# A fixed TensorE order re-spaced: where norm, the raw inputs and the fill steps stand, and when x is requested

## The chip, the core and the metric

The kernel runs on one core of a Trainium2 chip. A core has a matrix engine (TensorE, PE in the profile), a vector engine (VectorE, DVE), a scalar engine (ScalarE, ACT), a general engine (GpSimd, POOL) and SyncE (SP), which here issues the DMAs. Each engine works through its own queue in order; they wait for each other at semaphores. The metric is device time in microseconds.

## What is computed

One decoder layer with two branches beside each other, on x of 1024 rows by 1024 columns. The cut-down reference:

```python
h = rms_norm(x, pre_norm_gain)
proj = h @ w_in                                   # q, k, v of 3 attention groups, gates, RWKV inputs
# branch A: dilated sliding-window attention on q, k, v -> o_attn
# branch B: RWKV-7
pr = pr + (pr_prev - pr) * rwkv_shift_mix         # token shift, gives r, k, v, w_low, a_low
decay = exp(-exp(-softplus(-(w0 + tanh(w_low) @ w_up)) - 0.5))
a = sigmoid(a0 + a_low @ a_up)
kk = k * k_k;  kk = kk / max(norm(kk per head), 1e-12)
k = k * (1 + (a - 1) * k_a)
y = rwkv7_scan(r, decay, k, v, -kk, kk * a)       # delta-rule state update, token by token
o_rwkv = group_norm(y) * ln_w + ln_b + (sum(r * k * r_k)) * v
# merge
y_attn = (o_attn * silu(z_attn)) @ w_up_attn;  y_rwkv = (o_rwkv * silu(z_rwkv)) @ w_up_rwkv
merged = sigmoid(g_attn) * y_attn + sigmoid(g_rwkv) * y_rwkv
x = x + rms_norm(merged @ w_out, post_norm_gain)
```

## The kernel before

The work runs in stages: an opening (`start`), a small bias table, the RWKV branch (`rwkv`), attention, and the merge (`finish`).

The opening loads x in eight tiles of 128 rows, each by two DMAs that SP requests (L250, L251); the nine vectors of the layer (gains, mixes and so on) come by nine small DMAs into one tile `rows` (`vec_rows`, L298), which PE transposes once (L261). Each x tile is squared and summed (on ScalarE for the first four tiles, L276), scaled on DVE to `xn`, transposed by PE (L285), and split into a high part `hh` and a low part `hl` (L286, L287). All projections are then three fp32r matmuls per block of 128 rows of w_in: hi by hh, hi by hl, lo by hh. A weight block is requested by SP into `wstage`, its high part made on ScalarE or DVE (L135, L137) and the low part `wlo` on POOL (L138).

In the RWKV stage the sequence is cut into eight segments of 128 tokens. A segment has a preparation (`rwkv_prep`), transposed rows (`rwkv_rows`), the recurrence (`rwkv_chain`) and a group norm (`rwkv_post`), each written as a generator that does a step and yields. The steps of a preparation are:

- 1: requests of the raw k and r inputs of the segment, and their token shift on ScalarE and DVE (L506, L508);
- 2: the low-rank products (`wa` by `waup`), ScalarE's `sig` and `aa`, DVE's scan `c` (L528), POOL's `cm` (L529), ScalarE's `kk` and q = kk squared (L535);
- 3, called norm here: PE multiplies q by a head selector `hs`, DVE takes the maximum with 1e-24 into `rn` (L542), POOL raises it to the power -1/2 (L543);
- 4: PE transposes `rn`, DVE copies it to `rt` (L553), POOL makes `k`, half of `bk` and half of `ar`;
- 5: PE spreads `rt` over the heads, DVE and POOL finish `kk`, `ar` (L567) and `bk` (L569), `r` and the two `bw` tiles;
- 6 and 7: PE multiplies `ar` by `bk` into `gt` for half of the heads each, DVE evacuates with a mask (L590). Behind step 7 come the shift of v and `rwkv_blocks`: gt goes to DRAM (`tin_d`) and comes back as 16 by 16 blocks (`xinv`), 28 dependent DVE instructions (L617, L619) invert them, and they go to DRAM and back again (`x_d`, `xd`), where DVE transposes them to `xt` (L639);
- 8 to 11: PE completes the inverse (`pi`) from xt and gt.

`rwkv_rows` transposes `bw` for the two chunks of a segment (evacuated by ScalarE to `bkt`, L680 to L682), then v and r. `rwkv_chain` has for each of the two chunks three steps: rhs, upd (evacuated to `uv`, L724 on DVE and L725 on ScalarE), and snew.

PE has a fixed order through the whole RWKV stage (`keep_in_program_order`), written by hand: small steps with fill steps between them. A fill step is one matmul step of a projection that is due anyway (a pair of 256-column matmuls for the first 384 steps, then one of 512 columns), so that PE has work while the other engines answer. The order comes from three tables:

- `PROLOGUE`: pairs (what, number of fill steps behind it), before the loop over segments. "0", "1", "2" are the next step of that segment's preparation, "f" the next step of the first segment's rows. The first "0" is step 1 of segment 0, the second step 2, and so on.
- `LOOP`: pairs (what, weight), gone through once for each segment i. "C" is the next step of the chain, "f" of the next segment's rows, "t", "e", "a", "b" the next step of the preparation of segments i, i+1, i+2, i+3, "h" of the last segment's group norm. Behind each entry stand weight times `FILLS[i]` fill steps.
- `FILLS`: the number of fill steps per unit of weight, for each of the eight segments.

What is left of the fill steps after the loop follows in a row. On all other engines and queues the order is made by a scheduler that sees the whole program.

Of the kernel before, what the change touches and what calls it, by code (L numbers as in the profile page):

```python
# [34 lines left out]
C = 64  # L35
# [7 lines left out]

PROLOGUE = (("0", 24), ("0", 10), ("0", 10), ("0", 8), ("0", 44), ("0", 4), ("0", 4), ("1", 12), ("1", 16), ("1", 12),
            ("f", 4), ("f", 4), ("1", 8), ("1", 24), ("0", 8), ("0", 8), ("0", 8), ("1", 4), ("1", 6), ("0", 6), ("2", 0),
            ("f", 8))
LOOP = (("C", 0), ("t", 0), ("f", 1), ("a", 1), ("h", 1), ("C", 0), ("f", 1), ("a", 2), ("C", 0), ("a", 1), ("h", 2),
        ("C", 0), ("a", 1), ("f", 0), ("e", 2), ("C", 2), ("a", 1), ("e", 0), ("C", 1), ("a", 1), ("e", 1), ("b", 0))  # L50
FILLS = 6 * [6] + [5, 3]
CPS = SEG // C
KAPPA = math.exp(-0.5)
NEG = -1.0e30
# [58 lines left out]
class Kernel:  # L113
# [103 lines left out]
    def start(self):  # L217
        nc, tc, ctx, a = self.nc, self.tc, self.ctx, self.a
        pool = lambda **k: ctx.enter_context(tc.tile_pool(**k))
        self.cst = cst = pool(name="cst", bufs=1)  # L220
        self.wst = pool(name="wst", bufs=3)
        self.whl = pool(name="whl", bufs=3)
        self.ev = pool(name="ev", bufs=2)
        self.acc = pool(name="accp", bufs=2, space=PSUM)
        self.dram = pool(name="dram", bufs=1, space=DRAM)
        self.hstack = ExitStack()
        self.hpool = self.hstack.enter_context(tc.tile_pool(name="hT", bufs=1, side="right"))
        self.w_in = a["w_in"][0]
        self.sstack = ExitStack()
        self.small = self.sstack.enter_context(tc.tile_pool(name="small", bufs=1))  # L230

        self.ident = cst.tile([P, P], F32, name="ident")
        make_identity(nc, self.ident)
        self.eps = cst.tile([P, 3], F32, name="eps")
        nc.vector.memset(self.eps[:, 0:1], RMS_EPS)
        nc.vector.memset(self.eps[:, 1:2], GN_EPS)
        nc.vector.memset(self.eps[:, 2:3], 0.0)

        self.vecs = cst.tile([P, 49], F32, name="vecs")
        warm = cst.tile([P, 1], F32, name="warm")  # L240
        nc.scalar.activation(warm, self.eps[:, 2:3], AF.Sqrt)

        self.hT = []
        xr = a["x"][0].rearrange("(i r) d -> r i d", r=16)
        with tc.tile_pool(name="xin", bufs=1) as xin, tc.tile_pool(name="xps", bufs=5, space=PSUM) as xps:
            tiles = []

            def load(t):
                x = xin.tile([P, D], F32, name="x", tag="x", bufs=8)
                nc.sync.dma_start(x[0:64], xr[2 * t])  # L250
                nc.sync.dma_start(x[64:128], xr[2 * t + 1])  # L251
                tiles.append(x)

            rows = xin.tile([49, P], F32, name="rows")
            self.vec_rows(rows)
            for t in range(8):
                load(t)
                if t == 3:
                    self.w_wa = self.load_split(self.w_in, KT, OFF_WA)
            ps = xps.tile([P, 512], F32, name="xT", tag="xT")  # L260
            nc.tensor.transpose(ps[:, 0:49], rows, self.ident[0:49, 0:49])  # L261
            nc.vector.tensor_copy(self.vecs, ps[:, 0:49])
            self.small_loads()
            for half in range(2):
                hh = self.hpool.tile([P, KT, 512], F32R, name=f"hh{half}")
                hl = self.hpool.tile([P, KT, 512], F32R, name=f"hl{half}")
                self.hT.append((hh, hl))
                xs = []
                for j in range(4):
                    x = tiles[half * 4 + j]  # L270
                    sq = xin.tile([P, D], F32, name="sq", tag="sq", bufs=2)
                    st = xin.tile([P, 2], F32, name="st", tag="st", bufs=4)
                    if half:
                        nc.vector.tensor_tensor_reduce(sq, x, x, 1.0, 0.0, ALU.mult, ALU.add, st[:, 0:1])
                    else:
                        nc.scalar.activation(sq, x, AF.Square, accum_out=st[:, 0:1])  # L276
                    nc.scalar.activation(st[:, 1:2], st[:, 0:1], AF.Sqrt, bias=self.eps[:, 0:1], scale=1.0 / D)
                    nc.vector.reciprocal(st[:, 0:1], st[:, 1:2])
                    xn = xin.tile([P, D], F32, name="xn", tag="xn", bufs=5)
                    nc.vector.tensor_scalar(xn, x, st[:, 0:1], None, ALU.mult)  # L280
                    xs.append(xn)
                for k in range(KT):
                    ps = xps.tile([P, 512], F32, name="xT", tag="xT")
                    for j in range(4):
                        nc.tensor.transpose(ps[:, j * P:(j + 1) * P], xs[j][:, k * P:(k + 1) * P], self.ident)  # L285
                    nc.scalar.activation(hh[:, k], ps, AF.Copy, scale=self.gain[:, k:k + 1])  # L286
                    nc.vector.scalar_tensor_tensor(hl[:, k], ps, self.gain[:, k:k + 1], hh[:, k].bitcast(F32),  # L287
                                                   ALU.mult, ALU.subtract)
# [51 lines left out]
    def rwkv(self):  # L340
# [5 lines left out]
        with ExitStack() as ctx:  # L346
# [72 lines left out]
            def run(n):  # L419
                for _ in range(n):  # L420
                    next(fill, None)
# [4 lines left out]
            rows = self.rwkv_rows(0)  # L426
            for g, n in PROLOGUE:
                next(rows if g == "f" else prep[int(g)])
                run(n)
            for i in range(NSEG):  # L430
# [3 lines left out]
                work = dict(t=prep[i], e=prep[i + 1], a=prep[i + 2], b=prep[i + 3], f=rows, h=post)  # L434
                for g, n in LOOP:
                    if g == "C":
                        with tc.high_priority():
                            next(chain)
                    else:
                        next(work[g], None)  # L440
                    run(n * FILLS[i])
                for n in range(3 * i, 3 * i + 3):
# [712 lines left out]
```

## Time and profile before

| what | value |
|---|---|
| median of 3 runs | 1426.84 us (1419.84 to 1430.86) |
| the profiled execution's own time | 1421.31 us |
| its span | 1419.5 us |
| PE busy | 1333.9 us, 94% |
| DVE, ACT, POOL busy | 55%, 41%, 33% |
| mean granted TensorE clock | 0.986 |
| opening | 0 to about 36 us |
| prologue of the RWKV stage | about 92 to 185 us |
| loop over the eight segments | about 185 to 560 us, some 49 us a segment |

The profile is one execution, recorded by hardware. A row of a timeline has the start, the duration, the engine and line, the operation, and in brackets how long the engine had stood idle before it and what ended that. A row of the waits has an engine with its instruction, what it waited for, the sum, the number and the longest. The granted clock is 1.00 at 2.4 GHz and 0.50 at 1.2 GHz.

### The profile page before, as it was taken

The numbers are of one execution on the slowest core, as the hardware profiler recorded it, in microseconds if no ns is written. First come the engines' busy times: TensorE is split into PE (matmuls) and PEld (weight loads), VectorE is DVE, ScalarE is ACT, GpSimd is POOL, SyncE is SP. The second block draws the span as 40 slices with busy tenths as digits, with TensorE's granted clock in tenths as the row PEclk, the third lists the DMA queues.
The fourth block names the chain that finished last, engine by engine and source line by source line (L and its number), as shares of the span: only waits on it lengthen the run. The fifth ranks groups of instructions, "written<-read, shape, count | busy, mean of one in ns | idle before, by whom it ended". The sixth has DMA issues, their size and how long they took to land. (4 is left out here: it accounts for less than half of the span.)

```text
span 1419.5 us, 25770 instructions
## 1 busy us (share of the span) xinstructions
PE 1333.9 (94%) x10079; PEld 1115.3 (79%) x10079; DVE 779.9 (55%) x1676; ACT 576.4 (41%) x1378; POOL 475.4 (33%) x378
## 2 busy tenths in 40 slices
PE   5989899989999999999989998999899998999997
PEld 3989889767777777888878887888678876777886
DVE  5312657556464523565676557655766577338523
ACT  4444665564565332354425432643354320003211
POOL 1335644553355232322132213312222234433300
PEclk9999999999999999999999999999999999999999
DMA  7673544422322223111131112211221145654216
GB/s 175 184 217 107 135 107 101 114 68 74 100 77 74 62 75 94 45 41 34 43 101 35 48 40 75 62 44 41 62 67 31 45 152 176 200 169 150 62 38 171
DMA packets 192912, 131.17 MB, mean 92 GB/s; under 512 B 46421, under 2 KB 173022, under 8 KB 192790
## 3 DMA queue, kind: packets, MB, share of 16 engines
q1 hardware_dynamic: 192790, 129.52, 32.8%
q8 instruction: 79, 1.29, 0.4%
q14 instruction: 43, 0.35, 0.1%
HBM read 100.31 MB, written 33.89 MB: 95 GB/s over the span
## 5 line engine op out<-in xcount | busy, mean ns | idle before, releaser
L142 PE MATMUL acc<-hh,whi 128*128 128x512 f32 (+1 forms) x1360 | 480.3, 376 | 24.3 <-DVE kl L855 10.7
L142 PE MATMUL acc<-hh,wlo 128*128 128x512 f32 (+1 forms) x1360 | 470.2, 369 | 0.6 <-POOL wlo L138 0.6
L142 PE MATMUL acc<-hl,whi 128*128 128x512 f32 (+1 forms) x1360 | 470.0, 369 | 0.4 <-DVE hl L287 0.4
L138 POOL TENSOR_TENSOR wlo<-wstage,whi 128x512 fp32r<-128x512 f32 x186 | 247.6, 1332 | 527.2 <-DVE whi L135 244.1
L142 PEld LDWEIGHTS acc<-hh,whi 128*128 128x128 f32 x1360 | 246.8, 192 | 71.0 <-issue 15.8
L142 PEld LDWEIGHTS acc<-hh,wlo 128*128 128x128 f32 x1360 | 246.8, 191 | 38.7 <-POOL wlo L138 0.8
L142 PEld LDWEIGHTS acc<-hl,whi 128*128 128x128 f32 x1360 | 247.3, 192 | 36.2 <-issue 1.1
L875 ACT ACTIVATE L<-L,nm 128x128 f32<-128x128 f32 (+1 forms) x192 | 84.4, 441 | 86.1 <-DVE nm L872 85.8
L869 DVE CUSTOM_DVE_ANT_0 L<-pw,bias 128x128 f32<-128x128 f32 (+1 forms) x192 | 62.2, 350 | 50.3 <-PE pw L868 49.7
L854 POOL CAST k<-k 64x512 fp32r<-64x512 f32 x48 | 48.7, 1015 | 106.8 <-ACT k L853 98.2
L135 DVE CAST whi<-wstage 128x512 fp32r<-128x512 f32 x108 | 52.3, 486 | 51.3 <-PE acc L142 32.5
L853 ACT CAST k<-acc 64x512 fp32r<-64x512 f32 x48 | 43.0, 896 | 75.1 <-DVE kl L855 51.7
L137 ACT CAST whi<-wstage 128x512 fp32r<-128x512 f32 x78 | 48.6, 623 | 55.6 <-PE acc L142 24.7
L845 ACT ACTIVATE q<-acc 64x512 fp32r<-64x512 f32 x48 | 44.0, 916 | 56.1 <-DVE q L846 29.5
L855 DVE TENSOR_TENSOR kl<-acc,k 64x512 fp32r<-64x512 f32 x48 | 45.6, 950 | 33.5 <-ACT k L853 33.1
L617 DVE TENSOR_TENSOR xtmp<-xinv 64x14 f32<-64x14 f32 (+6 forms) x112 | 32.3, 288 | 46.7 <-DMA xinv<-tin_d 43.9
L846 DVE SCALAR_TENSOR_TENSOR q<-acc,q 64x512 fp32r<-64x512 f32 x48 | 45.0, 937 | 22.5 <-ACT q L845 21.6
L945 ACT CAST ph<-pw 128x512 fp32r<-128x512 f32 x72 | 40.9, 583 | 36.3 <-PE pv L954 22.0
L946 DVE TENSOR_TENSOR pl<-pw,ph 128x512 fp32r<-128x512 f32 x72 | 47.3, 670 | 11.9 <-ACT ph L945 10.6
L868 PE MATMUL pw<-kl,q 128*128 128x128 f32 (+1 forms) x192 | 50.6, 278 | 1.2 <-DVE kl L855 1.2
L1096 PE MATMUL acc<-wo,mh 128*128 128x512 f32 x128 | 50.4, 394 | 0.0
L1095 PE MATMUL acc<-wo,mh 128*128 128x512 f32 x128 | 50.2, 392 | 0.0
(232 smaller groups left out, 2173.7 us busy)
## 6 DMA issues: line engine op xcount, KB each, us to landing
wstage<-in_w_in_dram SPq DMA_DIRECT2D x170, 256.0 KB
x<-in_x_dram SPq DMA_DIRECT2D x32, 256.0 KB
raw<-raw_d SPq DMA_DIRECT2D x24, 258.0 KB
raw_d<-rv SPq DMA_DIRECT2D x24, 256.0 KB
wb<-wd SPq DMA_DIRECT2D x24, 256.0 KB
bias_d<-bias_r SPq DMA_DIRECT2D x24, 192.0 KB
tb_d<-tb SPq DMA_DIRECT2D x16, 256.0 KB
ga_d<-tb SPq DMA_DIRECT2D x16, 256.0 KB
```

What stands on the lines that cost most here:

```text
L135: self.nc.vector.tensor_copy(hi, x)
L137: self.nc.scalar.copy(hi, x)
L138: self.nc.gpsimd.tensor_tensor(lo, x, hi.bitcast(F32), ALU.subtract)
L142: ins = self.nc.tensor.matmul(*args, **kw)
L854: nc.gpsimd.tensor_copy(self.gview(ks2[h][b], g, half), hi.bitcast(F32))
L855: nc.vector.tensor_tensor(self.gview(kl[h][a], g, half), pv, hi.bitcast(F32), ALU.subtract)
L868: nc.tensor.matmul(ps[:, :w], qs2[h][:, qc], kl[h][:, kc], start=False, stop=True)
L869: nc.vector.tensor_tensor_reduce(l[:, l0:l0 + w], ps[:, :w], self.bias[h][:, bo:bo + w], 1.0, -3.0e38, ALU.add, ALU.max, st[:, gi, 0, h, n ...
L875: nc.scalar.activation(ls, ls, AF.Exp, bias=nm[:, n:n + 1], scale=1.0, accum_out=st[:, gi, 1, h, n:n + 1])
L946: nc.vector.tensor_tensor(pl[:, :cw], ps[:, :cw], ph[:, :cw].bitcast(F32), ALU.subtract)
L1095: nc.tensor.matmul(ps, mh[k][:, ts], wh[:, k], start=k == 0, stop=False)
L1096: nc.tensor.matmul(ps, mh[k][:, ts], wl[:, k], start=False, stop=False)
```

## The change

```diff
-PROLOGUE = (("0", 24), ("0", 10), ("0", 10), ("0", 8), ("0", 44), ("0", 4), ("0", 4), ("1", 12), ("1", 16), ("1", 12),
-            ("f", 4), ("f", 4), ("1", 8), ("1", 24), ("0", 8), ("0", 8), ("0", 8), ("1", 4), ("1", 6), ("0", 6), ("2", 0),
+PROLOGUE = (("0", 40), ("0", 16), ("0", 24), ("0", 8), ("0", 30), ("0", 8), ("0", 8), ("1", 20), ("1", 14), ("1", 12),
+            ("f", 12), ("1", 8), ("f", 4), ("1", 16), ("0", 8), ("0", 8), ("0", 8), ("1", 6), ("1", 6), ("0", 6), ("2", 0),
             ("f", 8))
-LOOP = (("C", 0), ("t", 0), ("f", 1), ("a", 1), ("h", 1), ("C", 0), ("f", 1), ("a", 2), ("C", 0), ("a", 1), ("h", 2),
-        ("C", 0), ("a", 1), ("f", 0), ("e", 2), ("C", 2), ("a", 1), ("e", 0), ("C", 1), ("a", 1), ("e", 1), ("b", 0))
-FILLS = 6 * [6] + [5, 3]
+LOOP = (("C", 0), ("t", 0), ("f", 1), ("a", 1), ("h", 1), ("C", 0), ("a", 1), ("f", 2), ("C", 0), ("a", 1), ("h", 2),
+        ("C", 0), ("a", 1), ("f", 0), ("e", 2), ("C", 0), ("b", 2), ("a", 1), ("e", 0), ("C", 1), ("a", 1), ("e", 1))
+FILLS = 4 * [6] + [6, 5, 4, 3]
...
             rows = xin.tile([49, P], F32, name="rows")
-            self.vec_rows(rows)
             for t in range(8):
                 load(t)
+                if t == 1:
+                    self.vec_rows(rows)
                 if t == 3:
                     self.w_wa = self.load_split(self.w_in, KT, OFF_WA)
```

Five things are in it. The nine vector requests stand behind x's second tile. The prologue's numbers of fill steps are other ones, 270 in all instead of 232, and one step of segment 1's preparation stands between the two first steps of rows. In the loop, norm (the second "a") stands directly behind the second chain step, before the second half of bw, with the two weights exchanged. The raw inputs of segment i+3 ("b") are requested behind the fifth chain step instead of at the end of the slot. `FILLS` has 5 and 4 for the sixth and seventh segment instead of 6 and 5. The number of fill steps is the same, 1056; 38 more stand in the prologue, 36 fewer in the two segments, two fewer behind the loop. From line 258 on, line numbers of the changed kernel are one higher.

On PE, in a segment of the loop, the steps behind the second chain step, upd (acc is a fill step, bw the transposes of the second chunk, hs,q is norm), stand so before:

```order
L142 MATMUL upd<-rhs_s,tt_440 64x64 x8
L148 MATMUL pg<-ident,bw 128x128 x4
L142 MATMUL acc<-hh_239,whi 128x512
L142 MATMUL acc<-hl_240,whi 128x512
L142 MATMUL acc<-hh_239,wlo 128x512
L142 MATMUL acc<-hh_153,whi 128x512
L142 MATMUL acc<-hl_154,whi 128x512
L142 MATMUL acc<-hh_153,wlo 128x512
L142 MATMUL pg<-hs,q 128x2 x4
```

and so in the changed kernel:

```order
L142 MATMUL upd<-rhs_s,tt_440 64x64 x8
L142 MATMUL pg<-hs,q 128x2 x4
L142 MATMUL acc<-hh_239,wlo 128x512
L142 MATMUL acc<-hh_239,whi 128x512
L142 MATMUL acc<-hl_240,whi 128x512
L142 MATMUL acc<-hh_239,wlo 128x512
L142 MATMUL acc<-hh_239,whi 128x512
L142 MATMUL acc<-hl_240,whi 128x512
L142 MATMUL pg<-ident,bw 128x128 x4
```

Norm's four small products have moved ahead of six fill steps and of bw's four transposes.

On DVE, at the same place of a segment, the maximum of rn (L542) and the copy uv of upd stand among the last instructions of an inverse (xtmp, xinv) so before:

```order
L724 COPY uv<-upd 64x4x64
L619 TENSOR_TENSOR xinv<-xinv,xtmp 64x10x5
L617 TENSOR_TENSOR xtmp<-xinv 64x44
L619 TENSOR_TENSOR xinv<-xinv,xtmp 64x11x4
L617 TENSOR_TENSOR xtmp<-xinv 64x36
L619 TENSOR_TENSOR xinv<-xinv,xtmp 64x12x3
L617 TENSOR_TENSOR xtmp<-xinv 64x26
L619 TENSOR_TENSOR xinv<-xinv,xtmp 64x13x2
L617 TENSOR_TENSOR xtmp<-xinv 64x14
L619 TENSOR_TENSOR xinv<-xinv,xtmp 64x14
L542 TENSOR_SCALAR rn<-pg 128x8
```

and so in the changed kernel:

```order
L725 COPY uv<-upd 64x4x64
L620 TENSOR_TENSOR xinv<-xinv,xtmp 64x11x4
L618 TENSOR_TENSOR xtmp<-xinv 64x36
L543 TENSOR_SCALAR rn<-pg 128x8
L620 TENSOR_TENSOR xinv<-xinv,xtmp 64x12x3
L618 TENSOR_TENSOR xtmp<-xinv 64x26
L620 TENSOR_TENSOR xinv<-xinv,xtmp 64x13x2
L618 TENSOR_TENSOR xtmp<-xinv 64x14
L620 TENSOR_TENSOR xinv<-xinv,xtmp 64x14
```

rn has moved from behind the last instruction of the inverse to the third place behind uv.

On POOL, in the prologue, the preparation of segment 0 from cm to the second half of ar (wlo are the low halves of weights) stands so before:

```order
L529 TENSOR_TENSOR cm<-c,sig 128x512
L543 TENSOR_TENSOR rn<-rn,mhalf 128x8
L561 TENSOR_TENSOR ar<-r,q 128x8x64
L707 TENSOR_TENSOR sw<-state,wc 128x256
L559 TENSOR_TENSOR k<-k,c 128x512
L138 TENSOR_TENSOR wlo<-wstage,whi 128x512
L560 TENSOR_TENSOR bk<-k,sig 128x8x64
L572 TENSOR_TENSOR r<-r,k 128x512
L138 TENSOR_TENSOR wlo<-wstage,whi 128x512
L567 TENSOR_TENSOR ar<-kk,cm 128x8x64
```

and so in the changed kernel:

```order
L530 TENSOR_TENSOR cm<-c,sig 128x512
L138 TENSOR_TENSOR wlo<-wstage,whi 128x512
L544 TENSOR_TENSOR rn<-rn,mhalf 128x8
L562 TENSOR_TENSOR ar<-r,q 128x8x64
L708 TENSOR_TENSOR sw<-state,wc 128x256
L138 TENSOR_TENSOR wlo<-wstage,whi 128x512
L560 TENSOR_TENSOR k<-k,c 128x512
L138 TENSOR_TENSOR wlo<-wstage,whi 128x512
L561 TENSOR_TENSOR bk<-k,sig 128x8x64
L573 TENSOR_TENSOR r<-r,k 128x512
L138 TENSOR_TENSOR wlo<-wstage,whi 128x512
L568 TENSOR_TENSOR ar<-kk,cm 128x8x64
```

Two more splits of weights stand between cm and the second half of ar, four instead of two.

## Rows read from the trace of the kernel before

**Rows 1.** The page, first part: busy time, share of the span, instructions.
```profile
PE 1333.9 (94%) x10079; PEld 1115.3 (79%) x10079; DVE 779.9 (55%) x1676; ACT 576.4 (41%) x1378; POOL 475.4 (33%) x378
```

**Rows 2.** PE's waits from 92 to 185 us: total, times, longest.
```profile
PE pg L142 <- ACT q L535: 8.6, 2, 5.5
...
PE pg L148 <- ACT bkt L681: 0.4, 1, 0.4
```

**Rows 3.** PE's waits from 185 to 570 us.
```profile
PE pg L148 <- POOL rn L543: 8.0, 6, 1.9
...
PE acc L142 <- DVE q L846: 2.4, 1, 2.4
PE pi L142 <- DVE xt L639: 1.5, 1, 1.5
```

**Rows 4.** Timeline of SP's requests in the opening: start, duration.
```profile
0.74 0.42 SPq L298 DMA_DIRECT2D rows<-in_pre_norm_gain_dram  x1
...
3.94 0.58 SPq L250 DMA_DIRECT2D x<-in_x_dram  x1
...
6.47 0.60 SPq L250 DMA_DIRECT2D x<-in_x_dram  x1
```

**Rows 5.** Timeline of ACT in the opening, the squares of tiles one and three.
```profile
8.96 1.06 ACT L276 ACTIVATE sq<-x 128x1024 f32<-128x1024 f32 x1 [6.73 <-DMA x<-in_x_dram]
...
13.45 1.06 ACT L276 ACTIVATE sq<-x 128x1024 f32<-128x1024 f32 x1 [0.77 <-DMA x<-in_x_dram]
```

**Rows 6.** Timeline of PE in the prologue.
```profile
108.05 0.37 PE L142 MATMUL pg<-hs,q 128*128 128x2 f32 x1 [5.54 <-ACT q L535]
...
128.29 0.68 PE L142 MATMUL pg<-ar,bk 64*64 64x64 f32 x30
...
144.85 0.38 PE L142 MATMUL pg<-hs,q 128*128 128x2 f32 x2 [3.05 <-ACT q L535]
...
165.11 0.50 PE L142 MATMUL pi<-xt,gt 64*64 64x64 f32 x9
```

**Rows 7.** Windows: length, busy time (and instructions) of each engine, granted clock, DMA.
```profile
145.21:152.04 6.83, 6.83 (x34) 6.83 (x34) 6.62 (x18) 5.48 (x14) 5.45 (x5) 0.50 0.38 113
561.63:565.04 3.41, 3.41 (x10) 2.64 (x9) 1.66 (x2) 1.06 (x1) 0.53 (x1) 0.50 0.55 154
...
159.20:165.10 5.90, 5.90 (x49) 5.77 (x48) 3.72 (x5) 3.66 (x7) 4.93 (x5) 1.00 0.59 141
537.70:547.00 9.30, 9.30 (x41) 7.63 (x42) 3.53 (x7) 1.32 (x3) 3.99 (x3) 1.00 0.18 58
```

**Rows 8.** Timeline of POOL in the prologue, segment 0.
```profile
106.92 1.27 POOL L529 TENSOR_TENSOR cm<-c,sig 128x512 f32<-128x512 f32 x1 [3.31 <-DVE c L528]
110.20 1.65 POOL L543 TENSOR_TENSOR rn<-rn,mhalf 128x8 f32<-128x8 f32 x1 [2.00 <-DVE rn L542]
...
119.83 1.30 POOL L567 TENSOR_TENSOR ar<-kk,cm 128x512 f32<-128x512 f32 x1
```

**Rows 9.** Timeline of DVE in the prologue.
```profile
122.95 0.69 DVE L569 SCALAR_TENSOR_TENSOR bk<-kk,sig 128x512 f32<-128x512 f32 x1
...
137.41 1.23 DVE L508 SCALAR_TENSOR_TENSOR v<-raw,vecs,v 128x128 f32<-128x128 f32 x4 [4.00 <-ACT v L506]
...
164.29 0.71 DVE L639 STREAM_TRANSPOSE xt<-xd 128x512 f32<-128x512 f32 x1 [1.40 <-DMA xd<-x_d]
```

**Rows 10.** Timeline of DVE in the fourth segment of the loop.
```profile
347.05 1.22 DVE L617 TENSOR_TENSOR xtmp<-xinv 64x54 f32<-64x54 f32 x1
...
348.54 0.20 DVE L617 TENSOR_TENSOR xtmp<-xinv 64x50 f32<-64x50 f32 x1
...
349.14 0.41 DVE L724 COPY uv<-upd 64x256 f32<-64x256 f32 x1
...
350.86 0.15 DVE L542 TENSOR_SCALAR rn<-pg 128x8 f32<-128x8 f32 x1
```

**Rows 11.** Timeline of POOL there.
```profile
346.91 1.28 POOL L138 TENSOR_TENSOR wlo<-wstage,whi 128x512 fp32r<-128x512 f32 x1
```

## The prediction

> **What bounds the kernel now.** The page's first part comes first: TensorE (PE) is busy 94% of the span [rows 1], so its gaps are all that a change of order can win, and they lie in places. The waits of PE by stretch lead to the tables that the change edits. In the prologue PE stands 8.6 us for q, the squared keys whose sums give norm, in two waits, and 0.4 us for a bkt evacuation [rows 2]; in the loop 8.0 us for rn, the power on POOL behind norm, in six waits and 1.5 us for xt once [rows 3]. The timelines of the first 20 us show the third place: PE can transpose nothing before x's tiles land, and those are asked for behind nine small requests [rows 4, 5]. Last the windows, for the granted clock: behind each of the two q waits there is a window of 6.83 us at 0.50, the 1.2 GHz level (the second stands in [rows 7]; the first, from 107.66, still holds 0.39 us of its wait). Full speed would save half of the rest: (6.83 - 0.39) / 2 + 6.83 / 2 = 6.6 us. So the two q waits cost 8.6 + 6.6 = 15.2 us, more than anything else here.
>
> All times below are on the profiled execution: 1421.3 us, 5.5 us under the median of the runs shown, 1426.8; the sum is made on the former and moved by 5.5 at the end.
>
> **Opening.** x's first request leaves SP at 3.94, nine row requests after 0.74; the third tile's first request at 6.47 [rows 4]. The change asks for tiles one and two first, four requests of (6.47 - 3.94) / 4 = 0.63 us, then the nine rows in 3.2 us. Tiles one and two are asked for 3.2 us earlier; tile three at 0.74 + 2.53 + 3.2 = 6.47, as before. ScalarE's squares start at 8.96 and 13.45 for tiles one and three, (13.45 - 8.96) / 2 = 2.24 us a tile: the transfers, not the requests, set that pace [rows 5]. With a head start tile two is in by 8.96 + 2.24 - 3.2 = 8.0, and tile three as long after its own request as tile one was: 6.47 + (8.96 - 3.94) = 11.49 instead of 13.45. What comes behind is a row of transfers at 2.24 us and follows: -2.0 us. The lower bound is nothing, if the weight stream later sets the start of the prologue anyway; the upper bound is the 3.2 us of the requests.
>
> **Prologue.** A fill step of two 256-column matmuls takes 5.90 / 24.5 = 0.241 us at full clock [rows 7] (49 matmuls). I keep the opening's shift out here.
> - First q: before it stand 56 fill steps instead of 34. PE came to norm at 108.05 - 5.54 = 102.51 [rows 6]; 22 x 0.241 = 5.3 us more make 107.8, so 0.2 us of 5.54 is left, and without a long wait I expect no half clock behind it.
> - First gt (the product of ar and bk): 118 steps stand before it, not 96. PE comes at 128.29 - 5.54 - 3.2 + 5.3 = 124.9 [rows 6]. bk was ready at 122.95 + 0.69 = 123.6 [rows 9], behind POOL's ar, which ended at 121.1 [rows 8]. Sixteen steps more, 3.9 us, stand ahead of the small product behind which cm is made; ScalarE and DVE lie between, and I take 3.0 of it, which puts cm at 109.9 instead of 106.92 [rows 8]. From cm's start to ar's end POOL took 121.1 - 106.9 = 14.2 us, 2.0 of them idle before rn; the order shows two more splits wlo there than before, 1.28 us each [rows 11]. 109.9 + 12.2 + 2.6 = 124.7 for ar, and bk as long behind it as before, 2.5 us: 127.2. **A new wait of 2.3 us**, which I take in two pieces (the weights' splits are late in the same queue), so without a drop of the clock. DVE's gt evacuations now stand among the shifts of v and k: seven such shifts are 7 / 4 x 1.23 = 2.2 us [rows 9], some of it beside PE's work between the pairs, and I take 0.9 for PE at the second pair. Bounds for the two: 0, where POOL's idle time swallows the splits, and 6, twice as much.
> - Second q: 168 steps before it, not 132. PE comes at 144.85 - 3.05 - 5.54 - 3.2 + 36 x 0.241 + 3.4 new = 145.1, after the 144.85 at which q was ready [rows 6]. No wait, no half clock.
> - First inverse product pi: 220 steps instead of 184. PE reached it at 165.11 without a wait; now at 165.11 - 15.2 + 8.7 + 3.4 = 162.0 [rows 6]. xt, its input, comes by two round trips to memory and 28 dependent DVE instructions; gt, their source, is no earlier than before, so xt stays at 164.29 + 0.71 = 165.0 [rows 9]. **A new wait of 3.0 us**, and since a wait of 2.4 us in the loop was followed by 3.41 us at half clock [rows 3, 7], half of the 1.7 us which that costs: 0.9.
>
> Together: 15.2 - 0.2 - 2.3 - 0.9 - 3.0 - 0.9 = **7.9 us gained**. Bounds: 3 and 15.2.
>
> The inverse's DVE instructions show what POOL does to them. An xtmp takes 0.20 us alone, and 1.22 us while POOL runs a wlo of 1.28 us [rows 10, 11]. So each split that falls into the 28-step chain puts xt back by 1.0 us, and the change puts splits closer to it; this speaks against the change and is part of rival two. The Trainium skill (SBUF — State Buffer, section "SBUF: two separate sides") states a cause: a DVE instruction with two SBUF inputs and a GpSimd instruction that reads SBUF use a port pair that one of them locks for its whole length. By that rule the 1.0 us is a wait for the lock, and the two rows agree with it; three more splits in the chain would make the prologue's gain 4.9 instead of 7.9.
>
> **Norm in the loop.** Norm now comes straight behind upd and before bw's second half; the steps from it to the transpose of rn grow from 12 to 18, while PE reaches the transpose at the same place. What decides is DVE's order: rn's maximum stood behind the whole inverse chain, ten places after uv, at 350.86, with uv at 349.14 [rows 10]; now it is the third after uv. 349.14 + 0.33 + 2 x 0.22 = 349.9, so 0.95 us earlier, and POOL and PE follow. Of 8.0 us in six waits [rows 3], four of 1.5 to 1.9 lose 0.95 each and the two small ones about 0.6 in all: -4.4 us. Bounds: 0 (POOL is the late one) and -8.0.
>
> **bw behind norm.** bkt's evacuation on ScalarE moves back and shares a pair of PSUM buffers with the next transposes. The nearest row is a bkt wait of 0.4 us [rows 2]; half of it in three segments, +0.6 us. Bounds: 0 and 2.4 (0.4 in six).
>
> **Raw inputs in slot four.** These are SP requests; their data is needed a segment later, some 49 us, and I cost them at nothing. If the cover were gone, it would be one request's wait on SP, and behind it stand only weight requests made steps ahead.
>
> **Thinner late segments.** 36 steps leave segments 5 and 6, counted from 0 (a full-width step is 9.30 / 41 = 0.227 us [rows 7]), 38 more stand in the prologue. The steps' own work is only moved. In segment 6, xt was 1.5 us late with five fills [rows 3]; about 12 of the 18 steps taken lie ahead of it, 12 x 0.227 = 2.7 us, shared with uv. Half of a clock drop adds 0.9, segment 5 0.4: **+4.0 us**. Bounds: 0, and 36 x 0.227 = 8.2.
>
> **Sum.** -2.0 - 7.9 - 4.4 + 0.6 + 4.0 = -9.7, so 1411.6 for an execution like the profiled one, and 1417 against the median.
>
> **Rivals.**
> 1. *All prologue waits go.* POOL's idle time takes the splits and xt comes early with gt. Then 15.2 instead of 7.9: 1417 - 7.3 = 1410. For it: POOL is free 3.3 and 2.0 us around cm [rows 8]. Against it: xt's route has no slack to PE.
> 2. *The bound only changes its name.* The waits for bk and xt come in one piece each, both with 3.4 us of half clock cost or 3 more splits in the chain: prologue 2 to 3 us instead of 7.9, and segments 5 and 6 cost 6: 1417 + 5 + 2 = 1424. For it: the 28-step chain with its instructions of 1.22 us [rows 10].
> 3. *Slower.* ScalarE's bkt, now behind four activations of another step, holds a PSUM buffer so long that PE's transposes wait 2.4 us or more in all six full segments, each followed by 3.41 us at half clock: 6 x (2.4 + 1.7) = 25 us, 1417 + 25 = 1442. It decides from about 2.4 us a segment, where the loop's row shows a drop [rows 3, 7]. Against it: the only bkt wait is 0.4 us.
> 4. *Nothing acts*: the waits move to the next step and the opening is hidden: 1427.
>
> **How the numbers follow.** The forecast holds 0.51, rival one 0.21, two 0.18, three 0.04, four 0.06. About 1% is what a measurement of this kernel tells from no change. Under 1412.6 lies most of rival one and the forecast's lower tail: 0.23. Over 1441 lies rival three: 0.04. Between: 0.73. The range goes from just past rival one, 1406, to rival four, 1427.
>
> **What would show it.** Right: ScalarE's third square near 11.5; no q wait over 0.5 us and no 6.83 us window at half clock in the prologue; a wait for bk or ar near 125 and one for xt near 163; the loop's waits for rn near 0.5 us; one longer xt wait in segment 6. Wrong: if PE's gaps from 92 to the loop's start do not shrink to about 7 us, the prologue term falls, and with it most of the gain; waits at rn that do not move say that POOL, not DVE's order, is late; a wait for bkt in each segment says rival three.

## The result, and the profile after

The changed kernel takes 1433.12 us (median of 6 runs, 1430.57 to 1434.49) against 1423.74 for the kernel before (median of 6). The ratio is 1.0067, its 95% interval 1.0044 to 1.0091: slower by 9.5 us, where 1417 us and a gain were forecast, and 6 us above the upper end of the range. The profiled execution took 1433.39 us, 12.1 more than that of before. Timelines of both say where: PE's first chain product stands 5.6 us later than before (190.9 against 185.3), with 38 more fill steps (9.2 us) ahead of it, so opening and prologue have gained 3.6. From there to the first product of attention PE takes 401.6 instead of 396.7 us, although 38 fill steps fewer stand in that stretch. All 38 are pairs, since the 384 pairs run out that much earlier (4562 products instead of 4639), 9.2 us of work: the loop and the stretch behind it have lost 14.1. Attention and merge take 1.5 us more.

The page of the changed kernel, first part (as [rows 1]):

```profile
PE 1339.1 (94%) x10079; PEld 1116.4 (78%) x10079; DVE 772.8 (54%) x1676; ACT 574.4 (40%) x1378; POOL 476.4 (33%) x378
```

PE's waits in its prologue, 92 to 192 us (as [rows 2]; total, times, longest):

```profile
PE pi L142 <- DVE xt L640: 2.8, 1, 2.8
PE pi L142 <- DVE xq L646: 2.3, 1, 2.3
PE pg L142 <- DVE bk L570: 1.9, 1, 1.9
PE pg L142 <- DVE gt L591: 1.6, 2, 1.0
```

The 8.6 us for q are gone, and in their place stand waits for bk, gt and xt, as forecast, and one for xq that was not. All its waits in this stretch come to 9.9 us, against 9.7 before; what the profiled prologue has gained is the clock, with one window of 3.41 us at half clock, from 172.3, in place of two of 6.83 [rows 7]:

```profile
172.32:175.73 3.41, 3.19 (x38) 3.08 (x39) 1.30 (x3) 2.07 (x6) 2.01 (x3) 0.50 0.95 296
```

PE's waits in the loop and behind it, 192 to 575 us (as [rows 3]):

```profile
PE pg L142 <- DVE kk L567: 11.7, 4, 6.6
PE acc L142 <- DVE q L847: 4.1, 1, 4.1
PE pg L142 <- ACT ys L762: 3.2, 1, 3.2
PE snew L142 <- ACT uv L726: 1.7, 2, 1.1
PE pi L142 <- DVE xt L640: 1.3, 1, 1.3
PE pg L148 <- POOL rn L544: 0.9, 2, 0.4
```

The waits for rn have shrunk from 8.0 to 0.9 us. The first line is new in size; before, it was:

```profile
PE pg L142 <- DVE kk L566: 3.3, 3, 1.9
```

The timeline of PE and the windows behind its longest waits (as [rows 6] and [rows 7]):

```profile
272.17 1.22 PE L142 MATMUL pg<-r,blk 128*128 128x512 f32 x1 [6.57 <-DVE kk L567]
...
421.45 1.21 PE L142 MATMUL pg<-r,blk 128*128 128x512 f32 x1 [4.03 <-DVE kk L567]
...
509.32 1.20 PE L142 MATMUL pg<-r,blk 128*128 128x512 f32 x2 [3.21 <-ACT ys L762]
```

```profile
267.89:278.13 10.24, 5.97 (x39) 3.96 (x40) 6.35 (x14) 6.55 (x19) 3.34 (x3) 0.50 0.47 130
421.49:424.91 3.41, 3.41 (x30) 1.91 (x32) 2.99 (x6) 3.06 (x10) 1.28 (x1) 0.50 0.10 20
510.24:517.07 6.83, 5.55 (x41) 4.26 (x40) 1.98 (x3) 1.39 (x5) 0.36 (x1) 0.50 0.26 83
```

In the profiled execution of before, no stretch of the loop's eight segments ran at half clock; now three do, each at a long wait. (It was a favourable one: run 8 below, with the same loop, has two such windows of 3.41 us, from 265.2 and 306.1.) The lines account for the loss. From the first chain product to attention PE's waits grew from 17.3 to 23.4 us, and of its work 5.97, 3.41 and 5.55 us ran at half clock, which costs half of it, 7.5 us: together 13.6 of the 14.1. Behind the first two stands one story, read from the timelines of DVE, then ScalarE, then SP in the second segment:

```profile
263.01 3.74 DVE L509 SCALAR_TENSOR_TENSOR k<-raw,vecs,k 128x128 f32<-128x128 f32 x4 [0.47 <-ACT k L507]
266.67 0.41 DVE L719 COPY rhs_s<-rhs 64x256 f32<-64x256 f32 x1
270.58 0.94 DVE L509 SCALAR_TENSOR_TENSOR v<-raw,vecs,v 128x128 f32<-128x128 f32 x3 [3.50 <-ACT v L507]
271.43 0.68 DVE L567 TENSOR_TENSOR kk<-kk,pg 128x512 f32<-128x512 f32 x1
```

```profile
270.14 1.28 ACT L507 ACTIVATE v<-raw,mix 128x128 f32<-128x128 f32 x4 [5.78 <-DMA raw<-raw_d]
```

```profile
266.78 0.37 SPq L505 DMA_DIRECT2D raw<-raw_d  x1
```

kk's input had been ready since 263.6, when PE ended its product of rt. But on DVE three of v's four shifts stand ahead of kk. They wait for ScalarE's part, that for a raw tile, and that tile is requested at 266.78, when k's shift has ended (263.01 + 3.74) and freed one of the two raw buffers. The transfer lands at 270.1, and kk comes at 271.43. PE's next product needs the buffer that kk empties.

### The profile page after: what moved, and what is told of

The parts are those of the page before. It is cut to its first block, busy times and chain, and to the rows that moved or that the text cites. A ratio compares the mean times of both kernels' runs of the same rounds, so it can differ in the third digit from the quotient of the medians.

```text
span 1431.6 us, 25779 instructions
## 1 busy us (share of the span) xinstructions
PE 1339.1 (94%) x10079; PEld 1116.4 (78%) x10079; DVE 772.8 (54%) x1676; ACT 574.4 (40%) x1378; POOL 476.4 (33%) x378
## 5 line engine op out<-in xcount | busy, mean ns | idle before, releaser
L142 PE MATMUL acc<-hh,whi 128*128 128x512 f32 (+1 forms) x1360 | 472.2, 370 | 24.3 <-DVE kl L856 10.8
L142 PE MATMUL acc<-hh,wlo 128*128 128x512 f32 (+1 forms) x1360 | 477.6, 374 | 1.3 <-POOL wlo L138 1.3
L1098 PE MATMUL acc<-wo,ml 128*128 128x512 f32 x128 | 50.3, 394 | 0.0
L1097 PE MATMUL acc<-wo,mh 128*128 128x512 f32 x128 | 50.2, 392 | 0.0
```

Of the source, the lines that this page charges most:

```text
L142: ins = self.nc.tensor.matmul(*args, **kw)
L1097: nc.tensor.matmul(ps, mh[k][:, ts], wl[:, k], start=False, stop=False)
L1098: nc.tensor.matmul(ps, ml[k][t // 4][:, cs], wh[:, k], start=False, stop=k == KT - 1)
```

## Experiments

Theory A: the earlier request of the raw inputs costs the most, not as a request but because k and r of a later segment now take the two raw buffers ahead of v, while DVE's order has v's shift in front of kk. Theory B: norm's new place does it. Theory C: the thinner segments do it. Each ratio is against the kernel before on the same chip, with its 95% interval.

**1. The raw inputs back at the end of the slot,** all else as changed.

```diff
-... ("C", 0), ("b", 2), ("a", 1), ("e", 0), ("C", 1), ("a", 1), ("e", 1))
+... ("C", 2), ("a", 1), ("e", 0), ("C", 1), ("a", 1), ("e", 1), ("b", 0))
```

> The changed kernel with one part undone: the raw inputs are requested at the end of the slot again. Theory A (the earlier request of the raw inputs is what costs: v's shift then stands ahead of kk on DVE and waits for a raw buffer): the waits of 6.57 and 4.03 us at PE's r,blk and their windows at half clock go, 11 + 5 us, so about 1418 us, and no wait for kk over 2 us. Theory B (norm's earlier place is what costs, by pushing bkt and kk back): the waits stay, 1431 to 1434 us. Theory C (the thinner late segments cost): also 1431 to 1434, with the two waits in place.

Measured: 1.0001 (0.9982 to 1.0019), 7 us better than the changed kernel by the medians, 9 by the two ratios; no wait for kk over 2.1 us. Theory A is right about its part, which is most of the slowdown, but the gain of the other parts is not there either: the time is that of before and not 1418.

**2. That part alone,** added to the kernel before.

```diff
-... ("C", 2), ("a", 1), ("e", 0), ("C", 1), ("a", 1), ("e", 1), ("b", 0))
+... ("C", 0), ("b", 2), ("a", 1), ("e", 0), ("C", 1), ("a", 1), ("e", 1))
```

> The kernel before with one part added: the raw inputs requested behind the fifth chain step. In its order v's shift stands ahead of kk on DVE in one segment only, the sixth, and by one instruction. Theory A: one new wait of about 4 us at r,blk there, with 3.41 us at half clock, and the others as before: about 1429 us. Theory B or C: as before, 1424 us, no wait for kk over 2 us.

Measured: 1.0047 (1.0022 to 1.0072), 6.7 us slower. Theory A's 1429 us came out as 1431.62. In its timeline of PE the wait stands in the one segment where a v shift is ahead of kk (the fifth; the expectation had miscounted):

```profile
425.20 0.77 PE L142 MATMUL pg<-r,blk 128*128 128x512 f32 x1 [3.84 <-DVE kk L566]
```

**3. The changed kernel, v's shift kept behind kk** on DVE and behind rhs_s on ScalarE.

```diff
-        shifted(2, v)
+        with tc.issue_after(kk_done.ins), tc.issue_after(self.rs_done.ins):   # from segment 2 on
+            shifted(2, v)
```

> The changed kernel with v's shift of each segment kept behind kk on DVE and behind rhs_s on ScalarE; everything else may move only as the scheduler then likes. Theory A: the waits for kk of 6.57 and 4.03 us fall under 1 us, 1418 to 1421 us. A rival of it (the earlier requests hurt as transfers, by their place in SP's queue or on the DMA engines): waits of the same size stay or turn up at xd and the weights, 1430 us or more.

Measured: 0.9975 (0.9956 to 0.9994), 11 us better than the changed kernel by the medians, 13 by the ratios, and 1.5 us over theory A's range. The same stretch on its DVE:

```profile
262.24 3.74 DVE L509 SCALAR_TENSOR_TENSOR k<-raw,vecs,k 128x128 f32<-128x128 f32 x4 [0.37 <-ACT k L507]
265.90 0.41 DVE L723 COPY rhs_s<-rhs 64x256 f32<-64x256 f32 x1
266.24 0.67 DVE L567 TENSOR_TENSOR kk<-kk,pg 128x512 f32<-128x512 f32 x1
```

k's shift takes the same 3.74 us; kk follows at once and PE waits 0.59 us instead of 6.57. The request is as early as in the changed kernel. So neither its transfer nor its place in SP's queue was the cost, but the place of v's shift.

**4. Norm's new place alone.**

```diff
-... ("f", 1), ("a", 2), ("C", 0) ...
+... ("a", 1), ("f", 2), ("C", 0) ...
```

> The kernel before with one part added: norm directly behind upd, weights exchanged. Theory A: the waits for rn fall from 8.0 to about 3.6 us in the loop and nothing else changes, 1419 to 1421 us against 1424. Theory B: new waits at r,blk or bkt of 4 us and more, 1430 us or more.

Measured: 0.9980 (0.9959 to 1.0001), a gain that is not clear of noise, and 1423.46 us lies between the two theories. PE's waits in its loop:

```profile
PE pg L148 <- ACT bkt L681: 3.3, 5, 1.1
...
PE pg L148 <- POOL rn L543: 1.7, 4, 0.4
```

rn falls from 8.0 to 1.7 us, more than expected, and bkt takes 3.3 of it back: rival three's mechanism, at 0.2 to 1.1 us a segment, far from the 2.4 at which it would have decided.

**5. The third kernel, with xinv in a buffer of its own.** In the seventh segment PE waits for ys, the group norm's output, which shared a buffer with xinv. The kernel also has one buffer for wa instead of two.

```diff
-        wa = self.rw.tile([P, SEG], F32, name="wa", tag="wa", bufs=2)
+        wa = self.rw.tile([P, SEG], F32, name="wa", tag="wa", bufs=1)
...
-        x = self.rw.tile([nb * nm, 16, 16], F32, name="xinv", tag="ys")
+        x = self.rw.tile([nb * nm, 16, 16], F32, name="xinv", tag="xinv")
```

> The third run's kernel (v's shift behind kk), and xinv in a buffer of its own instead of sharing one with the group norm's output ys. There PE waited 3.0 us for ys in the seventh segment and ran 6.83 us at half clock behind it. Theory A (ys waits for the inverse's last transfer because they share a buffer, and this is most of what the thinner segments cost): that wait and its window go, 3.0 + 3.4 us, about 1416 us against 1422.5. Rival (xt's round trip itself is what the thin segment cannot cover): the wait moves to pi behind xt, about 4 us there, and the time stays at 1421 to 1423.

Measured: 0.9990 (0.9963 to 1.0017), not better than the third run's 0.9975. The wait for ys is gone and stands two steps later:

```profile
505.14 0.59 PE L142 MATMUL pi<-xt,gt 64*64 64x64 f32 x6 [5.26 <-DVE xt L644]
```

So the wait has moved to xt, as the rival said: what the thin segment lacks is cover for xt's round trip, and the shared buffer made PE wait at an earlier instruction. The time is a weaker witness, since the second edit was not tried alone, and the waits for kk grew too (2.4 us in run 3, 4.6 here).

**6. The prologue's distances with the thinner segments, 7. the prologue's distances alone,** and **9. the thinner segments alone,** each added to the kernel before. Since the number of fill steps is fixed, the seventh kernel takes its 38 from behind the loop (all 32) and from the last segment.

```diff
 run 6:  PROLOGUE and FILLS of the changed kernel
 run 7:  PROLOGUE of the changed kernel, FILLS = 6 * [6] + [5, 3]
 run 9:  PROLOGUE of the kernel before,  FILLS = 4 * [6] + [6, 5, 4, 3]
```

> The kernel before with two parts added: the prologue's distances and the thinner segments; the loop's order is that of before. Theory A (the prologue gains about 8 us, the thin segments lose about as much): 1423 to 1427 us against 1425.7, PE's first chain step at about 9.2 - 8 = 1 to 4 us later than before, and all of the difference given back between the sixth segment and attention. The prediction's own terms: -7.9 + 3.4, 1421.

> The kernel before with the prologue's distances alone: the 38 fill steps then come from behind the loop (32) and the last segment (6), and segments five and six keep theirs. If the thin segments are what eats the prologue's gain: about 8 us less than before, 1417 to 1419. Rival (fill steps are worth as much wherever they are taken from, so that the end of the loop waits instead): 1424 to 1426, with longer waits in the last segment and at the first attention product.

> The kernel before with the thinner segments alone: the 36 fill steps taken from the sixth and seventh segment stand behind the loop instead, so PE's work is the same. If fill steps are worth there what the sixth and seventh runs say (8 to 11 us for 36 steps, less what more cover behind the loop saves, the 2.4 us wait with 1.7 us of half clock): 1429 to 1433 us against 1424. By the prediction's term (4.0 us, less the same): 1424.

Measured: run 6 1.0034 (1.0011 to 1.0056), run 7 1.0050 (1.0024 to 1.0076), run 9 1.0006 (0.9983 to 1.0029). Run 6 is 3 us over theory A's range, run 7 is slower than its rival too, by 6 us, and run 9 came out even, as by the prediction's term and not as by runs 6 and 7. So in runs 6 and 7 the kernel with the prologue's distances is slower than before, whether the segments or the end lend their fill steps. PE's waits from 440 to 620 us show who pays, first of run 6, then of run 7:

```profile
PE acc L142 <- DVE q L846: 4.2, 1, 4.2
PE pg L142 <- ACT ys L761: 3.4, 1, 3.4
PE snew L142 <- ACT uv L725: 2.7, 2, 1.4
```

```profile
PE acc L142 <- DVE q L846: 11.3, 1, 11.3
```

With nothing left behind the loop, PE stands 11.3 us for attention's first q instead of 2.4, and a window of 13.65 us at half clock, from 560.3, holds the end of that wait and 4.15 us of work. With thin segments it stands for ys, uv and q. Run 9, which has 68 steps behind the loop, does not wait for q at all and has no window at half clock there: 2.4 + 1.7 = 4.1 us saved, near the 4.9 that its segments lose (below), which would explain why it comes out even.

**8. The row requests behind x's second tile alone.**

```diff
-            self.vec_rows(rows)
             for t in range(8):
                 load(t)
+                if t == 1:
+                    self.vec_rows(rows)
```

> The kernel before with the nine row requests behind x's second tile and nothing else. The prediction's term: 2.0 us less, third square at 11.5 us. What the changed kernel's trace says: row requests are held up behind x's transfers, x's third tile is asked for at 8.3 instead of 6.5 us, the third square starts at 13.1, and the opening gains nothing: 1425 to 1426 us.

Measured: 1.0016 (0.9991 to 1.0041), no gain. In the changed kernel's opening (as [rows 4, 5]) SP and ScalarE show why, and run 8 has the same picture, its third square at 13.32:

```profile
4.90 0.29 SPq L299 DMA_DIRECT2D rows<-in_rwkv_k_k_dram  x1
5.57 0.25 SPq L299 DMA_DIRECT2D rows<-in_rwkv_k_a_dram  x1
6.67 0.25 SPq L299 DMA_DIRECT2D rows<-in_rwkv_r_k_dram  x1
7.65 0.25 SPq L299 DMA_DIRECT2D rows<-in_rwkv_ln_w_dram  x1
...
8.29 0.47 SPq L250 DMA_DIRECT2D x<-in_x_dram  x1
```

```profile
13.11 1.06 ACT L277 ACTIVATE sq<-x 128x1024 f32<-128x1024 f32 x1 [3.91 <-DMA x<-in_x_dram]
```

Ahead of x nine rows went out every 0.34 us. Behind four x requests three of them come 0.7, 1.1 and 1.0 us apart, and x's third tile is asked for at 8.29, not 6.47. Meanwhile the DMA engines stand idle for most of the time (the last columns of the windows are their mean busy share and GB/s):

```profile
6.00:8.00 2.00, 0.00 (x0) 0.00 (x0) 0.81 (x2) 1.37 (x4) 0.00 (x0) 1.00 0.29 56
8.00:10.00 2.00, 0.27 (x2) 0.21 (x2) 0.84 (x3) 1.16 (x3) 0.00 (x0) 1.00 0.23 37
```

**10. Norm alone, with c's activations behind bkt** on ScalarE, and **11. that with the row requests issued by ScalarE,** x first on SP.

```diff
 run 10:
+        with tc.issue_after(self.bkt_done.ins):   # from segment 2 on
             for p in pairs:
                 nc.scalar.activation(t[:, p], aa[:, p], AF.Identity, ...)
 run 11, also:
-            self.nc.sync.dma_start(rows[used:used + n], ...)
+            self.nc.scalar.dma_start(rows[used:used + n], ...)
```

> The fourth run's kernel (norm alone), with c's four activations of a segment kept behind bkt's evacuation on ScalarE. There PE's transposes of d waited 3.3 us for bkt in the loop, in five places. If these waits come from c standing ahead of bkt: they fall under 1 us and the time by up to 3, 1419 to 1421 against 1424 before. Rival (PE then waits for c's heirs, k and bk on POOL): the same time as norm alone, 1421 to 1423.

> The tenth run's kernel, with the nine row requests issued by ScalarE instead of SP, at the start, so that x's first request leaves SP at 0.74 and no row request stands ahead of any x request. If SP's order sets the opening: all four of the first squares about 3 us earlier than before (6, 8, 10.5, 12.5 us) and 2 to 3 us off the whole, 1417. If the transfers of the first 2 MB set it, or the weights behind them: squares earlier by at most 1 us, no change against the tenth run.

Measured: run 10 0.9974 (0.9950 to 0.9998). The loop's bkt waits are gone, but PE's waits for kk grow from 1.9 to 5.5 us, and against norm alone nothing clear is won: its rival is right about the time, though the wait that grew is for kk and not for k or bk. Run 11 1.0014 (0.9993 to 1.0035), some 6 us worse than run 10, where neither expectation had a loss. Its SP and ScalarE:

```profile
3.29 0.60 SPq L250 DMA_DIRECT2D x<-in_x_dram  x1
5.65 0.47 SPq L251 DMA_DIRECT2D x<-in_x_dram  x1
```

```profile
9.26 0.26 ACTq L298 DMA_DIRECT2D rows<-in_rwkv_ln_b_dram  x1
9.56 1.06 ACT L276 ACTIVATE sq<-x 128x1024 f32<-128x1024 f32 x1 [6.72 <-DMA rows<-in_rwkv_r_k_dram]
```

Now x's own requests stop after the fifth, and the rows on ScalarE are held up too, with the squares behind them. So the requests are held on either queue once enough of them are out, and not by their order on SP. It is not the bytes of four transfers that hold them: in the kernel before, eleven requests of 256 KB left SP from 3.94 to 10.21, 0.55 to 0.64 us apart, and only from 11.13 on did they come 1.1 us apart. A number of open requests would fit all three traces: nine are out in the changed kernel and in run 11 when the first is held, and eleven in the kernel before, of which the two of x's first tile had landed by 8.96. No run tried it.

**12. Norm, the earlier request and v's shift behind kk;** opening, prologue and fill steps as before.

> The kernel before with norm's new place, the raw inputs requested earlier, and v's shift kept behind kk and rhs_s; opening, prologue and fill steps as before. If the earlier request only did harm by v's place: not slower than norm alone, 1418 to 1422 against 1424. If it also hurts as traffic: 1426 or more, with waits at r,blk or xd.

Measured: 0.9957 (0.9937 to 0.9978), faster than both kernels. The earlier request costs nothing once v stands behind kk.

**13. One gate chunk more among the fill steps, 14. with the prologue's distances, 15. with the prologue's distances and run 12's order.** The chunk (48 steps) is drawn from the last stage, so that no segment has to lend anything.

```diff
 run 13:
-EARLY = 2
+EARLY = 3
 run 14:  also PROLOGUE of the changed kernel, FILLS = 6 * [6] + [5, 3]
 run 15:  run 14 and run 12
```

> Control: the kernel before with one projection chunk of the merge gate (48 fill steps, 11 us of PE's work) drawn from the last stage into the fill steps; they stand behind the loop, and nothing else is changed. If cover behind the loop saves the 2.4 us wait and its half clock: 3 to 4 us less, 1421 to 1423 against 1425. If the last stage needed that chunk as cover: 1425 to 1429.

> The kernel before with the prologue's distances and that extra chunk, so that the loop keeps all its fill steps and 42 stand behind it. If the prologue's 38 steps gain their 8.6 us whenever nobody else has to give them: 1416 to 1419 against 1425. If the prologue's gain is lost later for another reason than the missing fill steps (a later start of the loop's transfers, say): 1424 or more.

> The twelfth run's kernel (norm, the earlier request with v's shift behind kk) with the prologue's distances and the extra chunk. If the parts add up: 4 to 6 us for the twelfth run's, 6 to 9 for the prologue's, 1411 to 1415 against 1425. If the prologue's gain needs the thin segments: 1420.

Measured: run 13 0.9971 (0.9954 to 0.9988), run 14 0.9926 (0.9899 to 0.9953), run 15 0.9894 (0.9876 to 0.9911), each as its first theory had it (run 13 by its difference, 3.9 us). Against the control, the prologue's distances gain 0.9971 - 0.9926 = 0.45%, 6.4 us (5.6 by the medians, with only four runs of run 14), once the stretch behind the loop can lend the 38 steps and still keeps 42. Run 15 is the fastest of all, 1413.32 against 1428.12 us. PE's waits in its prologue are those of the changed kernel, and from 440 to 620 us these remain:

```profile
PE pi L142 <- DVE xt L643: 1.4, 1, 1.4
PE pv L958 <- ACT ph L949: 1.0, 1, 1.0
PE acc L142 <- DVE q L850: 0.8, 1, 0.8
```

## Why the prediction was wrong

The parts measured alone are 1.0016 (rows), 1.0034 (prologue with thinner segments), 0.9980 (norm) and 1.0047 (raw inputs): +0.77% together, near the measured +0.67%; each has an interval of about 0.2% on either side. Within that they add up, and each can be held against its term.

- **Opening, -2.0: no gain.** The step that failed is "tile three at 0.74 + 2.53 + 3.2 = 6.47, as before": it took the row requests' 0.34 us from a time when nothing was in flight. Behind four requests of x they were held, and tile three was asked for at 8.29. [rows 4] do not show that, but the same trace does a little later, where x's own requests come 1.1 us apart from 11.13 on. The term should have had the loss as its other bound.
- **Prologue, -7.9: right as a stretch, and not a gain of the kernel.** The q waits and their two windows at half clock went, the new waits are 1.9 for bk (2.3 forecast), 1.6 for gt (0.9) and 2.8 for xt (3.0); a wait of 2.3 for xq and a window of 3.41 us at half clock, from 172.3, stand where the term had "half of the 1.7 us". In eight profiles each (run 11 with its other opening aside), PE comes to the loop at 188.9 us on average with the old distances and at 189.3 with the new ones, which have 9.2 us more work ahead: 8.7 us gained. That it is near 7.9 is in part luck. Between the two profiled executions opening and prologue gained 3.6, and by the prediction's own sign, PE's gaps, the term would have fallen: they are 9.9 us where it wanted about 7. The average holds a wait for rt behind the first inverse, 0.7 to 5.3 us (2.9 on average) in the eight profiles with the old distances and in none with the new ones, and it was in no term. What failed is the next step, that the steps' own work is "only moved": runs 6 and 7 are slower than before, and run 14 gains 6.4 us where the stretch that lends has steps to spare.
- **Norm, -4.4 and +0.6: the mechanism right, the second term too small.** rn fell to 1.7 us in run 4 and to 0.9 in the changed kernel; bkt cost 3.3 in run 4, where I had taken half of one row's 0.4 three times. Net 0.20%, 2.8 us, against 3.8 forecast, with an interval that just takes in nothing.
- **Raw inputs, nothing: 6.7 us alone and 7.4 us in the changed kernel** (run 1, by the medians). This is the step that turned the sign. "These are SP requests; their data is needed a segment later ... I cost them at nothing" counts one request's wait. But a step of a preparation issues the shifts on ScalarE and DVE too, and k, r and v go through two raw buffers in program order: with k and r asked for ahead of v, v's tile waits for k's shift. The order on DVE, which could be seen beforehand, has shifts of v between the next segment's k and the kk that PE waits for in the second and the fifth segment of the changed kernel, exactly where its waits of 6.57 and 4.03 us stand, in one segment of run 2, and in none of runs 1, 3, 4 and 12. Run 3, which moves v's shift alone, wins 11 us by the medians.
- **Thinner segments, +4.0: too small, the least so alone (run 9).** From the second upd of the fifth segment to the first of the eighth, PE took 105.9 us before; with 36 fill steps (8.2 us) fewer it took 102.6 in run 9, 105.5 in run 1 and 108.7 in run 6: 4.9, 7.8 and 11.0 us lost; the changed kernel and runs 3 and 5 lie between (6.0, 5.8, 8.4). The eleven profiles without thin segments took 103.6 to 106.2. Run 6 has two windows of 6.83 us at half clock there, run 9 one; the first of run 6's began at 450.4, between waits of 1.38 and 1.77 us, and "half of a clock drop" did not hold that. Behind the loop the wait for q went from 2.4 to 4.1 us, with two fill steps fewer, in the changed kernel and in runs 1, 3, 5 and 6; that wait was in no term.

Rival three ended on the right side for a wrong reason; none of the rivals was v's shift. The forecast's own sum had a gain of 9.7 us, the measured loss is 9.5, 19.2 apart. By the single parts, prologue and thinner segments make 8.7 of it (4.8 lost in run 6 where 3.9 were to be won), the raw inputs 6.7, the opening 4.3 (2.3 lost, not clear of noise, where 2.0 were to be won) and norm 1.0, 20.7 in all.

Open in part: the last 1.5 us, which the profiled execution of the changed kernel takes longer in attention and merge, where PE's order is the same. PE worked 19.6 us at half clock there, 17.1 in that of before, which makes 1.3 of them; why one window, from 1189.5, is twice as long as its like before stays open.

## What to carry to other kernels

Where the other engines' order is a scheduler's, a moved step moves all that it issues: look at what now stands ahead of the instruction that frees the main engine's next buffer, and follow a ring of two buffers through the new order of its users. On an engine that is busy for 94% of the time filler work is lent and not made, so ask who lends it, and look for a stretch that doesn't wait (here the last stage, whose 48 steps let the same table gain 6.4 us). And before a term is taken from one profile, look whether that execution was a common one.

## What the runs showed of the hardware

The length of the inverse's chain goes by the number of its instructions that meet a wide GpSimd tensor operation. In eight profiles with the old prologue the first chain of 28 DVE instructions took 14.6 us with 5 instructions over 0.8 us (three profiles), 15.5 with 6, 16.7 with 7, and 17.7 with 8 (three): about 1.0 us for each, while the rest took 0.2. It is the same order of instructions on both engines each time; what differs is how the two stand to each other in time. In all seventeen profiles each of the 392 chain instructions over 0.8 us stands beside such an operation. The Trainium skill (SBUF — State Buffer, section "SBUF: two separate sides") describes an exclusive lock on a shared port pair that one instruction holds to its end, and these steps agree with it. The narrow operations do not: POOL's power steps, rn and sm on 128 by 8, take 1.65 us each and read SBUF, and of the 790 chain instructions that stand beside one of them alone, in all seventeen profiles, none took over 0.8 us. The profiled execution of before was one with 5: it waited 0.7 us for rt behind that chain. Run 2, whose prologue is the same, had 8:

```profile
164.70 0.57 PE L142 MATMUL pg<-rt,selp 8*128 8x128 f32 x1 [5.33 <-DVE rt L553]
```

So the profile on which the forecast stood was up to 4.6 us luckier in its prologue than others of the same order.

The other finding is the opening's: requests of 2 KB, whose own rows are 0.25 us, came up to 1.1 us behind the one ahead on SP (6.67 in the changed kernel) and 3.4 us on ScalarE (9.26 behind 5.87 in run 11) when nine or more had been sent. In the changed kernel the DMA engines' busy share was 0.29 and 0.23 in the 4 us from 6.00 on; in run 11 they stayed busy, and the squares queued behind the held request.
